# A hybrid decoder trunk on one Trainium2 core: the attention scores of token tile 1, all heads of a pair at once in four banks

## The chip, the cores and the metric

One core of one Trainium2 chip runs the whole program. The metric is the device time of one execution in microseconds (us); the median of several runs is compared. A profiled execution of the kernel before is at hand, and all rows below are from it.

The engines in this text: PE is the matrix engine, ACT the engine of activations and copies (ScalarE), DVE the vector engine, POOL the general one (GpSimd), SP the one that issues the loads. Each works through its own queue in the order in which the program gave it its instructions, and waits for the others by semaphores.

## The reference

Two decoder layers over 256 tokens and 1024 channels in float32. Each layer has a gated feed-forward block, a mixer of two parallel parts, a second feed-forward block and a small gated embedding. One part of the mixer is an mLSTM, the other an attention in which each query sees the 128 newest keys:

```python
def hybrid_layer(h, ...):
    h = h + 0.5 * swiglu(rmsnorm(h, ffn1_norm), ffn1_w_gate, ffn1_w_up, ffn1_w_down)
    z = rmsnorm(h, mix_norm) @ w_in            # mLSTM q k v o i f, attention q k v, two merge gates
    hm = mlstm_chunkwise(...)                  # q and k after a short convolution and SiLU
    ha = swa_gqa_sinks(aq, ak, av, a_sinks)
    h = h + (sigmoid(g_m) * (hm @ w_branch_m) + sigmoid(g_a) * (ha @ w_branch_a)) @ w_out
    h = h + 0.5 * swiglu(rmsnorm(h, ffn2_norm), ffn2_w_gate, ffn2_w_up, ffn2_w_down)
    return h + sigmoid(rmsnorm(h, ple_norm) @ ple_gate_w) * (p_i @ ple_proj_w)

def swa_gqa_sinks(q, k, v, sinks):             # 16 query heads, 4 key heads, blocks of 128 queries
    scores = einsum("bnqhgd,bnkhd->bnhgqk", qb, kw) / 8        # over two blocks of keys
    scores = where(valid, scores, -inf)        # 0 <= query - key < 128
    mx = maximum(max(scores), sink); pr = exp(scores - mx)
    den = sum(pr) + exp(sink - mx)
    return einsum("bnhgqk,bnkhd->bnqhgd", pr / den, vw)
```

## The kernel before

**Tiles.** The tokens are two tiles of 128, `t` = 0 and 1. Activations stand transposed, as channels by tokens. Every float32 factor is split into a high and a low half (`wh` and `wl` for weights, made by `feed` from the loaded `raw`: ACT casts `wh`, DVE subtracts to get `wl`), and a product is three matmuls: high by high, high by low, low by high. A weight part is 128 x 1024; PE needs both halves of a part when it reaches it. The weights ring has 8 parts.

**Order.** The text of the program is executed by a planner. `Clock` holds a model time for each engine from a few fixed costs; background work is written as Python generators (chains), each `yield` ends a stage, and `tick`, called between matmuls of the main jobs, advances every chain whose stage is done by the model time (`chain[1] <= self.clock.now`) and then feeds weight parts, if the model has ACT and DVE not too far behind. So what an edit of a chain does to the order reaches much further than the chain: the stages of all other chains and the weight parts fall to other places. The engines then follow the order as it was written down, whatever the true times are.

**The stretch in question** is the mixer, some 250 us per layer. PE's main jobs stand there in this order: `kvq` (attention q, k, v), `v` (mLSTM values), `gt` (merge gate A; four banks `gt`, read by ACT into `gate`), `if` (mLSTM gates; then `scans` on DVE, with an exponential and a logarithm on ACT), `z` (mLSTM q and k for two heads; two units of four weight parts each, followed by the convolution `conv`: four activations `cv` on ACT, 12 taps on DVE in two stages of six, a SiLU `cy` and a split `qk`), `ya` (the attention's output times its branch weights; reads the attention's result in `qT`), `og`, `z`, `gt`, `ym`, `yo`.

In the background run `scores` for each head pair `p` and tile `t` (started by `groups`), then two chains of `outputs`, each for four heads: exponential of the sink `es`, reciprocal of `dn`, scaling of `pr` on ACT, four transposes into a bank `tp`, split `ptd` (for tile 1 a second, masked `ptd` on DVE), the product `ha`, and its copy `hc`; when both halves of a pair are there, the result is split into `qT`. The decays of the mLSTM (`decays`: bank `wt`, exponentials `w`) run beside them. PSUM has 8 banks in one ring, `bank`, for all of this.

**`scores`** makes S = (t + 1) x 128 keys. A bank holds `per` = 512 / S heads: 4 for tile 0, 2 for tile 1. For tile 1 the loop over `j0` runs twice; each pass makes two banks (`sc`, one for each of two key heads `g`), then a copy of the newer block on ACT, the masked copy of the older block, the maxima on DVE, and the exponentials on ACT with their sums. The second pass begins after the exponentials of the first.

Of the kernel before, what the change touches and what calls it, by code (L numbers as in the profile page):

```python
# [14 lines left out]
AF = mybir.ActivationFunctionType  # L15
ALU = mybir.AluOpType
AX = mybir.AxisListType
PSUM = bass.MemoryType.PSUM

P = 128  # L20
# [12 lines left out]
NEG = -1e30  # L33
# [1228 lines left out]
class Swa:  # L1262
# [95 lines left out]
    def scores(self, t, p, acc, chains):  # L1358


        tr, nc = self.tr, self.nc
        S = (t + 1) * P
        per = NB // S
        tok = slice(t * P, (t + 1) * P)
        rows = [slice(g * AD, (g + 1) * AD) for g in range(2)]
        hd = [slice(4 * (2 * p + g), 4 * (2 * p + g) + 4) for g in range(2)]
        pr = tr.slot("pr")[:, : 8 * P].rearrange("p (g j s) -> p g j s", g=2, j=4)
        pr = [pr[:, g] for g in range(2)]
        mx, den = ([tr.col(n, 4) for _ in range(2)] for n in ("mx", "dn"))
        for j0 in range(0, 4, per):  # L1370
            js = slice(j0, j0 + per)
            ps = [tr.bank("sc").rearrange("p (j s) -> p j s", j=per) for _ in range(2)]
            for j in range(per):
                for x, y in ((0, 0), (0, 1), (1, 0)):
                    for g in range(2):
                        nc.tensor.matmul(ps[g][:, j, :], self.qT[x](4 * p + j0 + j, tok, p=rows[g]),
                                         self.kT[rows[g], y, p, :S], start=j + x + y == 0, stop=x == 1,
                                         skip_group_check=True)
            yield
            if t:  # L1380
                for g in range(2):
                    nc.scalar.copy(pr[g][:, js, :], ps[g][:, :, P:])
                yield
            for g in range(2):
                if t:
                    above = tr.above.bitcast(mybir.dt.uint32)[:, None, :].to_broadcast([P, per, P])
                    nc.vector.copy_predicated(pr[g][:, js, :], above, ps[g][:, :, :P])
                    nc.vector.tensor_reduce(mx[g][:, js], pr[g][:, js, :], axis=AX.X, op=ALU.max)
                else:
                    for j in range(per):  # L1390
                        i = j0 + j
                        nc.vector.tensor_tensor_reduce(pr[g][:, i, :], ps[g][:, j, :], tr.band, 1.0, NEG, op0=ALU.add,
                                                       op1=ALU.max, accum_out=mx[g][:, i : i + 1])
                nc.vector.scalar_tensor_tensor(mx[g][:, js], mx[g][:, js], -0.125, self.nsink[:, hd[g]][:, js],
                                               op0=ALU.mult, op1=ALU.min)
            yield
            for g in range(2):
                for j in range(per):
                    i = j0 + j
                    nc.scalar.activation(pr[g][:, i, :], pr[g][:, i, :], AF.Exp, scale=0.125, bias=mx[g][:, i : i + 1],  # L1400
                                         accum_out=den[g][:, i : i + 1])
        for g in range(2):
            chains.append(tr.later(self.outputs(t, p, g, acc, hd[g], pr[g], mx[g], den[g])))
            self.haT.written(chains[-1], 4 * p, 4, t)
# [76 lines left out]
```

## Time and profile before

| | |
|---|---|
| time, median of 3 runs | 1360.45 us (1360.2 to 1360.47) |
| the profiled execution | 1360.21 us, span 1358.5 us |
| matmuls / weight loads / DVE / ACT / POOL busy | 1350.4 / 1224.4 / 901.2 / 748.6 / 57.4 us |
| ACT table loads | 15, 1.283 us each |

The span runs from the first to the last instruction of the core. A timeline row has the start in us from the span's beginning, its length, engine, line, operation, output <- inputs with their sizes, and how many equal instructions follow each other in it (a row of several is as long as all of them); in brackets the idle time ahead of it and who ended it. A row of the waits gives who waited for whom: us in total, times, longest. Nearly every row has line 133, the recording helper, so work is told apart by its tiles. A matmul's row is longer than the time to the next one, since they overlap.

### The profile page before, as it was taken

Reading aid. Unit: us, or ns where it says so; the run is one execution under the profiler, and the core shown is the slowest. Engines: PE = TensorE matmul, PEld = TensorE weight load, DVE = VectorE, ACT = ScalarE, POOL = GpSimd, SP = SyncE. Lnnn points to the kernel's source line nnn. Section 1 sums busy time; section 2 is a strip of 40 time slices with the busy share of each in tenths; the row PEclk is TensorE's granted clock in tenths of the full one; section 3 lists DMA queues with packets and bytes.
Section 4 is the critical chain, followed back from the end, with each engine's and each line's share of the span. In section 5 each row is a group of like instructions: output and inputs, shape, how many; then the busy total and the mean of one; then the engine's idle time right before and its main releaser. Section 6 shows DMA issues by size and latency. Waiting matters only on the chain.

```text
span 1358.5 us, 22054 instructions
## 1 busy us (share of the span) xinstructions
PE 1350.4 (99%) x8990; PEld 1224.4 (90%) x8990; DVE 901.2 (66%) x1403; ACT 748.6 (55%) x1233; POOL 57.4 (4%) x82
## 2 busy tenths in 40 slices
PE   9999999999999999999999999999999999999998
PEld 7999887899899899988889998878998998999887
DVE  6766567888787655454666554578887876554545
ACT  6655446887565444443555443468875654444433
POOL 1000003000100000000000000020001000000000
PEclk9999999999999999999999999999999999999999
DMA  7655745355654475565466566463546554755651
GB/s 246 219 187 159 247 151 190 122 153 126 214 203 163 153 235 186 174 221 182 166 219 218 171 196 198 139 200 110 159 123 217 198 173 143 243 188 170 237 191 53
DMA packets 126789, 245.91 MB, mean 181 GB/s; under 512 B 15160, under 2 KB 24288, under 8 KB 126688
## 3 DMA queue, kind: packets, MB, share of 16 engines
q1 hardware_dynamic: 126672, 244.50, 55.7%
q8 instruction: 70, 1.15, 0.4%
q14 instruction: 31, 0.25, 0.1%
q10 hardware_dynamic: 16, 0.00, 0.0%
HBM read 242.39 MB, written 2.10 MB: 180 GB/s over the span
## 4 chain that ended last, share of the span: by engine, by line
PE 97%; DVE 2%; ACT 1%; issue 0%; DVEq 0%; ACTq 0%
PE dn L133 18%; PE pg L133 18%; PE pu L133 14%; PE gu L133 7%; PE gt L133 7%; PE z L133 7%; PE kvq L133 5%; PE ym L133 3%; PE og L133 3%; PE yo L133 3%; PE v L133 3%; PE tp L133 3%; PE ya L133 2%; PE sc L133 1%; DVE cv L133 1%; PE ha L133 1%
## 5 line engine op out<-in xcount | busy, mean ns | idle before, releaser
L133 DVE TENSOR_TENSOR wl<-raw,wh 128x1024 fp32r<-128x1024 f32 (+1 forms) x405 | 488.1, 1221 | 275.9 <-ACT wh L133 273.4
L133 ACT CAST wh<-raw 128x1024 fp32r<-128x1024 f32 x405 | 415.7, 1048 | 351.1 <-PE dn L133 68.8
L133 PE MATMUL dn<-wh,hid 128*128 128x512 f32 x688 | 218.1, 395 | 0.0
L133 PE MATMUL pg<-uT,wh 128*128 128x256 f32 x1088 | 195.0, 282 | 0.0
L133 PE MATMUL pu<-uT,wh 128*128 128x256 f32 x1088 | 193.9, 281 | 0.0
L133 PEld LDWEIGHTS pg<-uT,wh 128*128 128x128 f32 x1088 | 166.7, 188 | 0.3
L133 PEld LDWEIGHTS pu<-uT,wh 128*128 128x128 f32 x1088 | 166.3, 188 | 0.0
L133 PEld LDWEIGHTS dn<-wh,hid 128*128 128x128 f32 x688 | 129.2, 188 | 30.3
L133 PE MATMUL pg<-uT,wl 128*128 128x256 f32 x544 | 152.6, 280 | 0.0
L133 PE MATMUL pu<-uT,wl 128*128 128x256 f32 x544 | 152.5, 280 | 0.0
L133 PE MATMUL dn<-wl,hid 128*128 128x512 f32 x352 | 138.9, 395 | 0.0
L133 PEld LDWEIGHTS pg<-uT,wl 128*128 128x128 f32 x544 | 102.7, 189 | 0.0
L133 PEld LDWEIGHTS pu<-uT,wl 128*128 128x128 f32 x544 | 102.7, 189 | 0.0
L133 PE MATMUL gt<-uT,wh 128*128 128x256 f32 x512 | 92.8, 282 | 0.0
L133 PE MATMUL z<-uT,wh 128*128 128x256 f32 x512 | 92.6, 283 | 0.0
L133 PE MATMUL gu<-wh,uT 128*128 128x512 f32 x256 | 81.2, 398 | 0.6 <-ACT wh L133 0.4
L133 PEld LDWEIGHTS gt<-uT,wh 128*128 128x128 f32 x512 | 79.0, 188 | 1.5
L133 PEld LDWEIGHTS dn<-wl,hid 128*128 128x128 f32 x352 | 66.1, 188 | 15.3
L133 PEld LDWEIGHTS z<-uT,wh 128*128 128x128 f32 x512 | 78.8, 188 | 0.6
L133 ACT ACTIVATE wh<-raw,gcol 128x512 fp32r<-128x512 f32 (+1 forms) x104 | 58.9, 638 | 27.5 <-DMA raw<-in_ffn_w_gate_dram 16.1
L133 DVE SCALAR_TENSOR_TENSOR wl<-raw,gcol,wh 128x512 fp32r<-128x512 f32 (+1 forms) x104 | 62.5, 655 | 16.3 <-ACT wh L133 16.0
L133 PE MATMUL z<-uT,wl 128*128 128x256 f32 x256 | 71.9, 281 | 0.0
(221 smaller groups left out, 2178.2 us busy)
## 6 DMA issues: line engine op xcount, KB each, us to landing
raw<-in_w_in_dram SPq DMA_DIRECT2D x60, 1024.0 KB
raw<-in_ffn_w_up_dram SPq DMA_DIRECT2D x40, 1024.0 KB
raw<-in_ffn_w_down_dram SPq DMA_DIRECT2D x40, 1024.0 KB
raw<-in_ffn_w_gate_dram SPq DMA_DIRECT2D x38, 1024.0 KB
raw<-in_w_branch_a_dram SPq DMA_DIRECT2D x16, 512.0 KB
raw<-in_w_branch_m_dram SPq DMA_DIRECT2D x8, 1024.0 KB
raw<-in_w_out_dram SPq DMA_DIRECT2D x8, 1024.0 KB
raw<-in_ple_gate_w_dram SPq DMA_DIRECT2D x8, 1024.0 KB
```

The lines of the kernel that those rows point to most:

```text
L133: return issue(*args, **kw)
```

## The change

For tile 1 the two passes become one: the 24 score matmuls of a head pair stand in one block (they stood in two blocks of 12), in four banks at once instead of two and then two. Then come a stage of four copies on ACT, a stage of all masked copies and maxima on DVE, and a stage of all eight exponentials. Tile 0 has one pass as before; only the way in which its stages are written changes.

```diff
--- before.py
+++ after.py
@@ -1367,38 +1367,37 @@
         pr = tr.slot("pr")[:, : 8 * P].rearrange("p (g j s) -> p g j s", g=2, j=4)
         pr = [pr[:, g] for g in range(2)]
         mx, den = ([tr.col(n, 4) for _ in range(2)] for n in ("mx", "dn"))
+        banks = {}
         for j0 in range(0, 4, per):
-            js = slice(j0, j0 + per)
-            ps = [tr.bank("sc").rearrange("p (j s) -> p j s", j=per) for _ in range(2)]
+            banks[j0] = ps = [tr.bank("sc").rearrange("p (j s) -> p j s", j=per) for _ in range(2)]
             for j in range(per):
                 for x, y in ((0, 0), (0, 1), (1, 0)):
                     for g in range(2):
                         nc.tensor.matmul(ps[g][:, j, :], self.qT[x](4 * p + j0 + j, tok, p=rows[g]),
                                          self.kT[rows[g], y, p, :S], start=j + x + y == 0, stop=x == 1,
                                          skip_group_check=True)
+        yield
+        parts = [(slice(j0, j0 + per), g, ps[g]) for j0, ps in banks.items() for g in range(2)]
+        if t:
+            for js, g, ps in parts:
+                nc.scalar.copy(pr[g][:, js, :], ps[:, :, P:])
             yield
+        for js, g, ps in parts:
             if t:
-                for g in range(2):
-                    nc.scalar.copy(pr[g][:, js, :], ps[g][:, :, P:])
-                yield
-            for g in range(2):
-                if t:
-                    above = tr.above.bitcast(mybir.dt.uint32)[:, None, :].to_broadcast([P, per, P])
-                    nc.vector.copy_predicated(pr[g][:, js, :], above, ps[g][:, :, :P])
-                    nc.vector.tensor_reduce(mx[g][:, js], pr[g][:, js, :], axis=AX.X, op=ALU.max)
-                else:
-                    for j in range(per):
-                        i = j0 + j
-                        nc.vector.tensor_tensor_reduce(pr[g][:, i, :], ps[g][:, j, :], tr.band, 1.0, NEG, op0=ALU.add,
-                                                       op1=ALU.max, accum_out=mx[g][:, i : i + 1])
-                nc.vector.scalar_tensor_tensor(mx[g][:, js], mx[g][:, js], -0.125, self.nsink[:, hd[g]][:, js],
-                                               op0=ALU.mult, op1=ALU.min)
-            yield
-            for g in range(2):
-                for j in range(per):
-                    i = j0 + j
-                    nc.scalar.activation(pr[g][:, i, :], pr[g][:, i, :], AF.Exp, scale=0.125, bias=mx[g][:, i : i + 1],
-                                         accum_out=den[g][:, i : i + 1])
+                above = tr.above.bitcast(mybir.dt.uint32)[:, None, :].to_broadcast([P, per, P])
+                nc.vector.copy_predicated(pr[g][:, js, :], above, ps[:, :, :P])
+                nc.vector.tensor_reduce(mx[g][:, js], pr[g][:, js, :], axis=AX.X, op=ALU.max)
+            else:
+                for j in range(4):
+                    nc.vector.tensor_tensor_reduce(pr[g][:, j, :], ps[:, j, :], tr.band, 1.0, NEG, op0=ALU.add,
+                                                   op1=ALU.max, accum_out=mx[g][:, j : j + 1])
+            nc.vector.scalar_tensor_tensor(mx[g][:, js], mx[g][:, js], -0.125, self.nsink[:, hd[g]][:, js],
+                                           op0=ALU.mult, op1=ALU.min)
+        yield
+        for g in range(2):
+            for j in range(4):
+                nc.scalar.activation(pr[g][:, j, :], pr[g][:, j, :], AF.Exp, scale=0.125, bias=mx[g][:, j : j + 1],
+                                     accum_out=den[g][:, j : j + 1])
         for g in range(2):
             chains.append(tr.later(self.outputs(t, p, g, acc, hd[g], pr[g], mx[g], den[g])))
             self.haT.written(chains[-1], 4 * p, 4, t)
```

The number of matmuls, DVE instructions and ACT instructions other than table loads stays. Where they stand in the queues changes through the planner, in both layers alike. Three places, in the first layer (numbers behind names are the program's own and differ between the two orders):

ACT's queue at the job `gt`, before: the exponentials of tile 1, pair 1 (`pr` with `mx`), the copies of its scores and the gates.

```order
L133 CAST wh_3124<-raw_2986 128x1024
L133 ACTIVATE pr_3036,dn_3039<-pr_3036,mx_3037 128x128 x2
L133 ACTIVATE pr_3036,dn_3040<-pr_3036,mx_3038 128x128 x2
L133 COPY pr_3036<-sc_3144 128x256
L133 COPY pr_3036<-sc_3145 128x256
L133 CAST wh_3174<-raw_3061 128x1024
L133 COPY hc_3183<-ha_3168 64x512
L133 CAST wh_3185<-raw_3061 128x1024
L133 ACTIVATE gate_3200<-gt_2888 128x512
L133 ACTIVATE gate_3200<-gt_2889 128x512
L133 COPY hc_3183<-ha_3217 64x512
L133 ACTIVATE pr_3036,dn_3039<-pr_3036,mx_3037 128x128 x2
```

The same place after the change:

```order
L133 COPY pr_2993<-sc_3012 128x256
L133 COPY pr_2993<-sc_3013 128x256
L133 CAST wh_3052<-raw_2852 128x1024
L133 COPY hc_2972<-ha_3043 64x512
L133 ACTIVATE es_3062<-es_3062 128x4
L133 ACTIVATE es_3064<-es_3064 128x4
L133 CAST wh_3083<-raw_2852 128x1024
L133 ACTIVATE gate_3149<-gt_2835 128x512
L133 ACTIVATE gate_3149<-gt_2836 128x512
L133 ACTIVATE pr_2993,dn_2996<-pr_2993,mx_2994 128x128 x4
L133 ACTIVATE pr_2993,dn_2997<-pr_2993,mx_2995 128x128 x4
L133 CAST wh_3166<-raw_3081 128x1024
```

All eight exponentials now stand behind the two `gate` activations, and with them `qT` and the scaling of tile 0 (`pr` with `dn`); four of them stood ahead of the gates.

DVE's queue at the job `z`, before: the taps `cv` of the first unit (`z` is its bank), the masked `ptd`, and the weight halves `wl` near them.

```order
L133 TENSOR_TENSOR wl_3438<-raw_3306,wh_3437 128x1024
L133 TENSOR_TENSOR ptd_3446<-tp_3432,ptd_3446 128x512
L133 TENSOR_TENSOR ptd_3497<-ptd_3430,upto 128x512 x2
L133 SCALAR_TENSOR_TENSOR cv_3465<-z_3302,feat_2151,cv_3465 128x255
L133 SCALAR_TENSOR_TENSOR cv_3465<-z_3302,feat_2151,cv_3465 128x254
L133 SCALAR_TENSOR_TENSOR cv_3465<-z_3302,feat_2151,cv_3465 128x253
L133 SCALAR_TENSOR_TENSOR cv_3468<-z_3303,feat_2151,cv_3468 128x255
L133 SCALAR_TENSOR_TENSOR cv_3468<-z_3303,feat_2151,cv_3468 128x254
L133 SCALAR_TENSOR_TENSOR cv_3468<-z_3303,feat_2151,cv_3468 128x253
L133 TENSOR_TENSOR rows_93<-nM_3301,rows_93 4x384
L133 TENSOR_TENSOR ptd_3525<-ptd_3446,upto 128x512 x2
L133 TENSOR_TENSOR wl_3482<-raw_3306,wh_3481 128x1024
```

After the change:

```order
L133 TENSOR_TENSOR ptd_3388<-tp_3367,ptd_3388 128x512
L133 TENSOR_TENSOR hc_3381<-ha_3383,hc_3381 64x512
L133 SCALAR_TENSOR_TENSOR cv_3441<-z_3268,feat_2151,cv_3441 128x255
L133 SCALAR_TENSOR_TENSOR cv_3441<-z_3268,feat_2151,cv_3441 128x254
L133 SCALAR_TENSOR_TENSOR cv_3441<-z_3268,feat_2151,cv_3441 128x253
L133 SCALAR_TENSOR_TENSOR cv_3444<-z_3269,feat_2151,cv_3444 128x255
L133 SCALAR_TENSOR_TENSOR cv_3444<-z_3269,feat_2151,cv_3444 128x254
L133 SCALAR_TENSOR_TENSOR cv_3444<-z_3269,feat_2151,cv_3444 128x253
L133 TENSOR_TENSOR rows_93<-nM_3267,rows_93 4x384
L133 TENSOR_TENSOR ptd_3477<-ptd_3386,upto 128x512 x2
L133 TENSOR_TENSOR ptd_3486<-ptd_3388,upto 128x512 x2
L133 TENSOR_TENSOR wl_3490<-raw_3275,wh_3489 128x1024
```

`wl_3490` is the low half of the sixth of the eight weight parts of `z`. In the order before, `wl_3438` and `wl_3482` at the same place belong to `ya`; all parts of `z` stand further ahead, the sixth ahead of the scans. Now the taps, `rows` and both masked `ptd` pairs stand between the scans and the sixth part of `z`.

ACT's queue between `z` and `ya`, before: `cy` is the SiLU, `em` and `w` are exponentials, which need another table.

```order
L133 ACT_TABLE_LOAD
L133 ACTIVATE cy_3620<-cv_3465 128x512
L133 ACTIVATE cv_3629<-z_3471,feat_2151 128x256 x2
L133 ACTIVATE cv_3632<-z_3472,feat_2151 128x256 x2
L133 ACTIVATE cy_3646<-cv_3468 128x512
L133 ACT_TABLE_LOAD
L133 ACTIVATE em_3654<-gcols_3588 128x8
L133 CAST qk_3658<-cy_3620 128x512
L133 CAST qk_3660<-cy_3646 128x512
L133 CAST qT_140<-hc_3558 128x4x128
L133 ACTIVATE w_3681<-wt_3656,gcols_3588 128x128 x3
```

After the change:

```order
L133 ACT_TABLE_LOAD
L133 ACTIVATE cy_3549<-cv_3441 128x512
L133 ACT_TABLE_LOAD
L133 ACTIVATE em_3566<-gcols_3538 128x8
L133 CAST qk_3570<-cy_3549 128x512
L133 ACT_TABLE_LOAD
L133 ACTIVATE cy_3572<-cv_3444 128x512
L133 CAST wh_3578<-raw_3494 128x1024
L133 CAST qT_140<-hc_3535 128x4x128
L133 CAST wh_3598<-raw_3494 128x1024
L133 ACT_TABLE_LOAD
L133 ACTIVATE w_3590<-wt_3568,gcols_3538 128x128 x3
```

The two `cy` stood together in one table; they now stand apart, with exponentials between them, and each change of function has a table load. The whole order has 23 of them, where the one before has 15: four more in each layer, all behind the logarithm.

## The prediction

> **What bounds the kernel now.** I read the page first, then the waits of the matrix engine (PE), the busy times of the mixer's middle, and its timelines.
>
> ```profile
> span 1358.5 us, 22054 instructions
> PE 1350.4 (99%) x8990; PEld 1224.4 (90%) x8990; DVE 901.2 (66%) x1403; ACT 748.6 (55%) x1233; POOL 57.4 (4%) x82
> PE 97%; DVE 2%; ACT 1%; issue 0%; DVEq 0%; ACTq 0%
> ```
>
> PE is busy for 99% of the span and is 97% of the chain that ended last. The change keeps PE's 8990 matmuls, so it can gain little more than PE's idle time, 1358.5 - 1350.4 = 8.1 us; it can lose whatever PE is made to wait.
>
> ```profile
> PE ya L133 <- DVE wl L133: 0.9, 2, 0.5
> 285.00:305.00 20.00, 20.00 (x172) 20.00 (x171) 16.95 (x36) 16.46 (x38) 0.00 (x0) 1.00 0.56 142
> 305.00:325.00 20.00, 20.00 (x163) 19.49 (x162) 17.06 (x32) 12.33 (x21) 0.00 (x0) 1.00 0.59 124
> ```
>
> The first row is from the waits, the others from the busy times in stretches (PE, weight loads, DVE, ACT, POOL, granted clock, DMA share, GB/s). In the middle of the mixer DVE is busy 17 of each 20 us and ACT 12 to 16. This is the one stage where these two nearly set the pace: `ya` already waits for a `wl` half, once per layer (0.9 us, 2 times). An order that makes them idle for some us here can't win that back.
>
> **The change part by part.** The work on each engine is equal but for the table loads below. What counts is where the planner now puts it.
>
> *1. Joined score blocks (a gain).* Two blocks of 12 score matmuls become one of 24, twice per layer.
>
> ```profile
> 240.97 0.98 PE L133 MATMUL sc<-kT,qT 64*128 64x256 f32 x12
> 241.87 0.50 PE L133 MATMUL v<-wh,uT 128*128 128x512 f32 x1
> 251.92 1.09 PE L133 MATMUL ha<-ptd,vv 128*128 128x512 f32 x4
> 252.85 0.40 PE L133 MATMUL v<-wh,uT 128*128 128x512 f32 x1
> 274.51 0.60 PE L133 MATMUL tp<-ident,pr 128*128 128x128 f32 x4
> ```
>
> Twelve take 0.90 us from start to start. Entering and leaving a block shows as a matmul's 0.50 where 0.40 is usual, and as much ahead: 0.2 us a joint. Two joints, and some transposes that now stand side by side, save 0.7 us per layer (between 0 and 1).
>
> *2. Banks.* The four score banks and the four of `gt` are all eight. Six `gt` matmuls later the order has `ha_3043`, which needs a score bank back: a copy on ACT and a masked copy on DVE must end first, on DVE behind a `wl` split of 1.2 us. Between 0 and 1.2 us; I take 0.8, as both engines have other work in front.
>
> *3. Wait A, at the `z` weights.* ACT's queue now has the two `gate` activations ahead of the eight exponentials of tile 1 (first place shown in the order); before, four of these stood ahead of the gates. ACT stands idle until PE ends the bank of `gt_2835`, and all behind it starts then.
>
> ```profile
> 281.43 2.85 PE gt L133 x24
> 290.91 8.51 PE z L133 x72
> 301.01 7.80 PE z L133 x66
> ```
>
> These are rows of the chain that ended last. The 24 are the 133rd to 156th `gt` matmul; the bank is full with the 138th: 281.4 + 6 x 0.118 + 0.2 for the result = 282.3. By the order of the changed kernel PE has two blocks of transposes less ahead of it (the row at 274.51, 0.60 with a tail of about 0.25, so 0.35 each), a pair of `ha` (half of 0.93) and two joints (0.4), 1.6 us together, and the 0.8 of the bank more: 281.5, say 281.4.
>
> ```profile
> 232.16 0.40 ACT L133 ACTIVATE pr<-pr,mx 128x128 f32<-128x128 f32 x1
> 235.26 0.62 ACT L133 COPY pr<-sc 128x256 f32<-128x256 f32 x2
> 271.49 2.45 ACT L133 ACTIVATE pr<-pr,dn 128x128 f32<-128x128 f32 x8
> 283.25 1.09 ACT L133 ACTIVATE gate<-gt 128x512 f32<-128x512 f32 x2
> 286.94 1.99 ACT L133 CAST wh<-raw 128x1024 fp32r<-128x1024 f32 x2
> 289.79 0.61 ACT L133 CAST qT<-hc 128x512 fp32r<-128x512 f32 x1
> 290.30 0.30 ACT L133 ACTIVATE es<-es 128x4 f32<-128x4 f32 x2
> 293.73 1.28 ACT L133 ACT_TABLE_LOAD   x1
> 295.02 0.42 ACT L133 ACTIVATE gates<-gates 4x256 f32<-4x256 f32 x1
> 301.32 0.59 ACT L133 CAST ptd<-tp 128x512 fp32r<-128x512 f32 x1
> ```
>
> ACT then runs, by its order, without a pause to the logarithm of the gates (start to start, in us): gates 1.05, eight exponentials 3.10 (232.16 to 235.26), `wh` 1.0, `qT` 0.5, eight scalings 2.4, `wh` 1.0, `es` 0.2, gates 1.05, `wh` 1.0, two `ptd` 1.0, `wh` 1.0, eight scalings 2.4, exponential 0.4, table 1.28, logarithm 0.42: 17.8. So it ends at 299.2, where before it ended at 295.44.
>
> ```profile
> 288.00 2.36 DVE L133 TENSOR_TENSOR wl<-raw,wh 128x1024 fp32r<-128x1024 f32 x2 [1.56 <-ACT wh L133]
> 295.47 0.41 DVE L133 SCALAR_TENSOR_TENSOR gates<-gates,gates 4x256 f32<-4x256 f32 x1
> 299.14 1.21 DVE L133 TENSOR_TENSOR wl<-raw,wh 128x1024 fp32r<-128x1024 f32 x1
> 302.59 0.69 DVE L133 TENSOR_TENSOR ptd<-tp,ptd 128x512 fp32r<-128x512 f32 x1
> 303.19 1.29 DVE L133 TENSOR_TENSOR ptd<-ptd,upto 128x512 fp32r<-128x512 f32 x2
> 304.39 2.93 DVE L133 SCALAR_TENSOR_TENSOR cv<-z,feat,cv 128x255 f32<-128x255 f32 x6
> 307.34 0.55 DVE L133 TENSOR_TENSOR rows<-nM,rows 4x384 fp32r<-4x384 f32 x1
> ```
>
> DVE goes on (second place in the order): the scans 3.67 (295.47 to 299.14), `wl` 1.2, two `hc` and two `ptd` at 0.6 (302.59 to 303.19), six taps of `cv` 2.95, `rows` 0.55, four masked `ptd` 2.4 (1.2 a pair), `wl_3490` 1.2: 14.4, so 313.6. PE needs `wl_3490` in the sixth of eight weight parts of `z`. In the order before, the sixth part is split by 290.4 (the row at 288.00), 16 us ahead. PE gets there after 120 `z` matmuls: 72 and 6 (not shown), then 42 of the 66, 301.0 + 5.0 = 306.0, and two matmuls with the high half follow at 306.2. The work ahead of it is the same in both orders, so in the changed kernel 306.2 + 0.8 - 0.7 = 306.3. Wait A: 7.3 us; the summed queues are good to a tenth of 32 us, so 4 to 10. Rows that follow each other overlap by up to 0.1, so the sum is a little long; I take 6.8.
>
> *4. Wait B, at the `ya` weights.* Exponential and SiLU need different tables. The order has 23 table loads where the page's groups had 15: four more per layer, all after the logarithm (third place).
>
> ```profile
> L133 ACT ACT_TABLE_LOAD x15 | 19.2, 1283 | 5.0 <-DVE cv L133 3.4 <-PEq L1470 1.4
> 302.47 1.93 ACT L133 ACTIVATE cv<-z,feat 128x256 f32<-128x256 f32 x4 [0.56 <-PE z L133]
> 317.82 0.63 ACT L133 ACTIVATE cy<-cv 128x512 f32<-128x512 f32 x1
> 322.22 1.12 ACT L133 CAST qk<-cy 128x512 fp32r<-128x512 f32 x2
> 323.77 0.87 ACT L133 ACTIVATE w<-wt,gcols 128x128 f32<-128x128 f32 x3
> ```
>
> After A ends at t, PE does 4 `z`, 8 `ha` (first four done at t + 1.7), the small transposes, 66 `z`, two `wt`, 50 `ya`: 0.5 + 1.9 + 0.3 + 7.8 + 0.6 + 5.9 + 0.5 for joints = 17.5 until `ya` needs `wl_3665`. ACT, starting from `ha`: two copies to t + 3.2, then `wh` 1.0, four tables 5.1, two `cy` 1.1, two `qk` 1.0, `qT` 0.5, two `wh` 2.0, `w` 0.8, first `cv` pair 0.95: t + 15.65; DVE then six taps 2.95 and the split 1.2: t + 19.8. Wait B is 2.3 (0 to 4). The next part, `wl_3682`, follows six more taps and a split, 4.15 later, while PE has 3.3 of work: wait C, 0.85. Without the two extra tables of this stretch (2.6 us), B would be nothing. The other two load while ACT has time.
>
> *5. The clock after A.*
>
> ```profile
> 1354.00:1356.00 2.00, 0.35 (x3) 0.14 (x2) 0.85 (x2) 0.38 (x1) 0.00 (x0) 1.00 0.02 7
> 1356.00:1358.50 2.50, 0.00 (x0) 0.00 (x0) 0.00 (x0) 0.00 (x0) 0.00 (x0) 0.60 0.15 52
> 1.68 2.32 PE L568 MATMUL heat<-heat 128*128 128x512 bf16 x5 [1.68 <-DVE heat L563]
> 5.55 0.59 PE L568 MATMUL heat<-heat 128*128 128x512 bf16 x2
> ```
>
> PE ends at 1354.35, and the granted clock falls to a mean of 0.60 in the last 2.5 us, so about 2 us of rest lower it. At the start 512 columns take 0.46 us, by 5.55 about half; the slow spell lasts 2.3 to 3.9 us. A wait of 6.8 us should set this off; the PE then loses half the spell, 1.2 to 1.9 us. C and B could hide it, but their `ha` is slowed as well. I take 1.5 (0 to 2) per layer. The Trainium skill's TensorE: Matmul & The Clock Gate, section Why this matters for your kernels, warns of gaps over about 3 us. By that rule B's 2.3 lowers nothing and A does, which is the sum as it stands.
>
> **Sum per layer:** bank 0.8, A 6.8, B 2.3, C 0.85, clock 1.5, less the joints 0.7 and the old `ya` wait 0.45: 11.1. Both layers have the same order, so 22.2. The profiled execution took 1360.21 (1.7 us outside the span), 0.24 below the median of the three runs: 1360.45 + 22.2 = 1382.7, say 1383.
>
> **The rivals.**
> - *The clock stays up:* 1383 - 3 = 1380. The end of the trace speaks against it.
> - *A is hidden.* If ACT's and DVE's queues regain their lead before `z`, B, C and bank remain without the clock: 2 x (0.8 + 2.3 + 0.85 - 1.15) = 5.6, so 1366. For it: DVE is 3 us of 20 idle before. Against: the idle time stands ahead of the gates, and the queue behind is unbroken by the order.
> - *The lag goes on:* ACT reaches the `og` weights and the mLSTM heads late too, one more wait like B and C: 2 x 5, so 1393. For it: four loads too many; against: in the second half of `ya` its order holds little but weight halves.
> - *A table load costs twice its row*, by a stall around it: 1.28 more for one load in A and four in B, 2 x 6.4 more, 1396. Against: the load at 293.73 is followed by the logarithm at 295.02, 1.29 later. The Trainium skill's ScalarE: Activation LUTs, section What ACT_TABLE_LOAD costs, adds a drain of about 1.38 us to each load; this trace has none.
> - *Not slower.* Only the joints count: 1360.45 - 2 x 1.15 = 1358. This needs the queue from the gates to `wl_3490` to run in 24.9 us instead of 32.2; it decides at 306.3. That is 23% off a sum of measured rows.
>
> **How the numbers follow.** Forecast with the clock's fall 0.5, without it 0.25, hidden A 0.08, lag that goes on 0.11, dear table loads 0.02, not slower 0.04. Likeliest is 1383. With A at 4 and no clock it is 1374, A at 10 gives 1389; with a part of the hidden case below and the lag above, 1370 to 1394. A change under 0.2% (2.7 us) can't be told from none: faster 0.02, same 0.02, slower 0.96.
>
> **What would show it.** PE's waits would list `z` behind DVE `wl`, twice, 5 to 8 us each, and `ya` behind DVE `wl` at 2 to 3; the granted clock would dip near 315 and 995. ACT should idle 3 to 5 us ahead of `gate`. The table loads would count 23. If `z` doesn't wait, or PE's idle time stays near 8 us, the argument is wrong.

## The result, and the profile after

The changed kernel takes 1386.03 us (median of 4 runs, 1385.51 to 1386.65) against 1360.43 for the kernel before: 1.0186 times as long, with a 95% interval of 1.0174 to 1.0198. It is 25.6 us slower, where the forecast had 22.2; the time lies inside the forecast range, 1383 (1370 to 1394). The profiled execution took 1385.95, with a span of 1384.2: 25.7 more than before.

The page, the table loads from its groups, and the waits of PE (what PE waited for and which engine ended it; us in total, times, the longest):

```profile
span 1384.2 us, 22068 instructions
PE 1354.4 (98%) x8990; PEld 1226.6 (89%) x8990; DVE 900.5 (65%) x1403; ACT 758.8 (55%) x1241; POOL 49.9 (4%) x82
PE 93%; DVE 3%; ACT 2%; issue 0%; DMA 0%; SPq 0%; ACTq 0%
L133 ACT ACT_TABLE_LOAD x23 | 29.5, 1283 | 10.7 <-DVE cv L133 9.0 <-PEq L1469 1.4
PE z L133 <- DVE wl L133: 12.9, 2, 6.5
PE ya L133 <- DVE wl L133: 7.2, 6, 2.1
PE ha L133 <- DVE pr L133: 1.9, 2, 1.0
PE gu L133 <- ACT wh L133: 1.2, 2, 1.0
```

The work is the same, 8990 matmuls. PE's idle time is 1384.2 - 1354.4 = 29.8 us where it was 8.1, and DVE and ACT now hold 5% of the chain that ended last, where they held 3%. The list names the places: once per layer `z` waits 6.5 us for a weight half, `ya` waits three times, `ha` waits 1.0 for a score bank.

The first layer in the timelines, PE's rows first:

```profile
274.32 1.20 PE L133 MATMUL ha<-ptd,vv 128*128 128x512 f32 x4 [0.97 <-DVE pr L133]
314.24 0.58 PE L133 MATMUL z<-uT,wl 128*128 128x256 f32 x1 [6.43 <-DVE wl L133]
315.26 3.62 PE L133 MATMUL ha<-ptd,vv 128*128 128x512 f32 x8
328.74 0.38 PE L133 MATMUL ya<-qT,wl 128*128 128x256 f32 x1 [0.76 <-DVE wl L133]
337.07 0.39 PE L133 MATMUL ya<-qT,wl 128*128 128x256 f32 x1 [2.15 <-DVE wl L133]
341.05 0.39 PE L133 MATMUL ya<-qT,wl 128*128 128x256 f32 x1 [0.72 <-DVE wl L133]
282.02 1.25 ACT L133 ACTIVATE gate<-gt 128x512 f32<-128x512 f32 x2 [4.62 <-PE gt L133]
295.10 2.45 ACT L133 ACTIVATE pr<-pr,dn 128x128 f32<-128x128 f32 x8
297.88 1.28 ACT L133 ACT_TABLE_LOAD   x1
299.17 0.42 ACT L133 ACTIVATE gates<-gates 4x256 f32<-4x256 f32 x1
312.97 1.22 DVE L133 TENSOR_TENSOR wl<-raw,wh 128x1024 fp32r<-128x1024 f32 x1
331.48 1.96 ACT L133 ACTIVATE cv<-z,feat 128x256 f32<-128x256 f32 x4
331.81 0.63 DVE L133 TENSOR_TENSOR wt<-wt,mask_st 128x128 f32<-128x128 f32 x2 [1.39 <-PE wt L133]
```

The brackets give the idle time ahead of a row and what ended it. ACT rests 4.62 us ahead of the gates, the logarithm ends at 299.6 (forecast 299.2), `wl_3490` is split at 314.2 (forecast 313.6), and PE, idle since 307.8, goes on at 314.24. The same weight part was split by 290.4 before: it now comes 24 us later. The last two rows are ahead of the second wait at `ya`: DVE's masking of `wt` waits 1.39 us for PE.

Stretches around that wait (busy us of PE, weight loads, DVE, ACT, POOL; then the granted clock, DMA share, GB/s):

```profile
310.00:312.00 2.00, 0.00 (x0) 0.00 (x0) 1.99 (x4) 0.00 (x0) 0.00 (x0) 1.00 0.00 0
312.00:313.00 1.00, 0.00 (x0) 0.00 (x0) 1.00 (x3) 0.00 (x0) 0.00 (x0) 0.83 0.00 0
313.00:319.00 6.00, 4.76 (x14) 3.53 (x15) 4.50 (x9) 0.67 (x2) 0.00 (x0) 0.50 0.53 128
319.00:320.00 1.00, 1.00 (x9) 0.98 (x9) 0.46 (x2) 0.97 (x2) 0.00 (x0) 0.76 1.04 201
```

At half speed the clock stands for 0.34 + 6 + 0.48 = 6.8 us. It falls near 312.7, 4.9 us after PE went idle, and is back near 319.5, 5.2 us after PE went on; the eight `ha` in that spell take 3.62 us.

### The profile page after: what moved, and what is told of

Same layout as the page of the kernel before. It is cut to its first block, busy times and chain, and to the rows that moved or that the text cites. A ratio compares the mean times of both kernels' runs of the same rounds, so it can differ in the third digit from the quotient of the medians.

```text
span 1384.2 us, 22068 instructions
## 1 busy us (share of the span) xinstructions
PE 1354.4 (98%) x8990; PEld 1226.6 (89%) x8990; DVE 900.5 (65%) x1403; ACT 758.8 (55%) x1241; POOL 49.9 (4%) x82
## 3 DMA queue, kind: packets, MB, share of 16 engines
q8 instruction: 70, 1.15, 0.3%
## 4 chain that ended last, share of the span: by engine, by line
PE 93%; DVE 3%; ACT 2%; issue 0%; DMA 0%; SPq 0%; ACTq 0%
PE dn L133 17%; PE pg L133 17%; PE pu L133 14%; PE gu L133 7%; PE gt L133 6%; PE z L133 5%; PE kvq L133 5%; PE ym L133 3%; PE og L133 3%; PE yo L133 3%; PE v L133 3%; PE ya L133 2%; PE tp L133 2%; DVE cv L133 1%; PE ha L133 1%; DVE wl L133 1%
```

## The experiments

All ratios are to the kernel before, run on the same chip beside each (medians of 1360.60 to 1360.76).

**tables: no switching of tables.** SiLU of the mLSTM convolution is left out, Tanh stands in its place; the planner still counts it as SiLU, so the order stays.

```
-        nc.scalar.activation(y, acc.rearrange("p c t -> p (c t)"), AF.Silu)
+        y_in = acc.rearrange("p c t -> p (c t)")
+        tr.clock.charge("scalar", NB, AF.Silu)
+        tr.tc.nc.scalar.activation(y, y_in, AF.Tanh)
```

> The order of the changed kernel, instruction for instruction, but the last activation of the mLSTM convolution (cy) is issued as Tanh, which shares its table with the exponential; SiLU of the convolution is left out. The extra table loads of the middle are gone, so the loads fall well under 15. Theory 1 (step 4 of the prediction): the table loads make the waits at ya; without them the three waits of 0.76, 2.15 and 0.72 us per layer go, 1386.0 - 2 x 3.6 = 1378.8, at least the 2.15, 1381.7. Theory 2: the wait of 2.15 is set by DVE, whose masking of wt waits 1.39 us for PE's own wt at 331.4 and has 0.6 + 0.6 + 2.9 + 1.2 us behind it until wl; then only the 0.76 behind the first ya goes, all behind it moves with PE, the waits of 2.15 and 0.72 stay: 1386.0 - 1.5 = 1384.5. The wait at z stays at 6.4 under both, since only one load, that of the logarithm, lies ahead of it and stays.

Measured: 1384.50 us, ratio 1.0173 (1.0158 to 1.0188). The page lists 9 table loads (7 and 2, on two lines of the kernel) where the changed kernel has 23. PE's waits, PE's row of wait B, and DVE ahead of it:

```profile
PE z L133 <- DVE wl L133: 12.9, 2, 6.5
PE ya L133 <- DVE wl L133: 5.9, 4, 2.2
337.51 0.39 PE L133 MATMUL ya<-qT,wl 128*128 128x256 f32 x1 [2.24 <-DVE wl L133]
332.25 0.63 DVE L133 TENSOR_TENSOR wt<-wt,mask_st 128x128 f32<-128x128 f32 x2 [3.92 <-PE wt L133]
332.79 0.68 DVE L133 TENSOR_TENSOR qk<-cy,qk 128x512 fp32r<-128x512 f32 x1
333.39 2.93 DVE L133 SCALAR_TENSOR_TENSOR cv<-z,feat,cv 128x255 f32<-128x255 f32 x6
336.24 1.22 DVE L133 TENSOR_TENSOR wl<-raw,wh 128x1024 fp32r<-128x1024 f32 x1
```

Theory 2 holds. The 0.76 goes, the 2.15 stays as 2.24. With 14 loads less DVE only rests longer, 3.92 us, in front of the masking of `wt`, which waits for PE's own `wt`; the split that `ya` needs stands behind that mask and six taps. So wait B (the 2.15) is a fixed distance in DVE's queue behind a PE instruction. The median falls by 1.5 us, and the intervals of the two kernels overlap. That is not the price of the 14 loads alone: in the first layer the clock stays at half speed twice as long here (last section), so that from the `z` matmul to the first `ya` PE takes 329.02 - 313.89 = 15.13 us where the changed kernel takes 327.54 - 314.24 = 13.30. The spans of the two profiled executions differ by 1.2 us; with this 1.83 added, the loads are worth about 3 us, an estimate. Of the 3.92 us of rest, at least about 2.1 would be left without the longer spell, so the mask would wait for PE all the same.

**fill44 and fill20: PE kept busy in the wait.** Matmuls with a zero weight, 44 in one run and 20 in the other, are put ahead of the `z` matmul that waits; they add nothing to `z`. The main lines, as in fill44:

```
                     mm(o, part.hi[:, kk - k0, cc], xT[1](kk), start=False, stop=False, **kw)
+                    if base == "z" and c == 0 and kk == 2:
+                        self.fills += 1
+                        for _ in range(44 if self.fills % 4 == 2 else 0):
+                            self.tc.nc.tensor.matmul(o, self.zero, xT[0](kk), start=False, stop=False, **kw)
```

> The changed kernel with 44 matmuls with a zero weight, 0.118 us each, that add nothing to z, put ahead of the z matmul that waits for wl in each layer: PE is busy for 5.2 of the 6.43 us that it waits. Theory 1: the clock falls because PE rests; it then stays at 1.00, the 6.83 us at 0.5 are gone, the wait at z is listed as 1.2, and PE gains most of the 2.6 us per layer: 1386.0 - 5.2 = 1380.8, and up to 1382 if a part is given back. Rival 1: the lost clock was hidden anyway, the waits at ya grow from 3.6 to 6.2 per layer: 1386. Rival 2: the clock falls for another reason: 0.5 is there again after the wait, 1386.

> As fill44 with 20 zero matmuls, 2.4 us, at the front of the wait: PE rests for 4.0 us behind them instead of 6.43. In the changed kernel the clock fell 4.9 us after PE had gone idle. Theory 1: it falls only after about that much rest, so here it stays at 1.00 and the time is that of fill44, 1381 to 1382. Rival: a rest of about 3.4 us (half of the 6.83 us that the record shows at 0.5) or less is enough, the clock falls to 0.5 as before, the time stays at 1386.

Measured: fill44 1382.17 us, 1.0156 (1.0141 to 1.0171); fill20 1385.84 us, 1.0183 (1.0168 to 1.0198). PE's rows of fill44 with one of its stretches, then of fill20 with two:

```profile
307.41 5.30 PE L504 MATMUL z<-uT,zero 128*128 128x256 f32 x44
314.00 0.38 PE L133 MATMUL z<-uT,wl 128*128 128x256 f32 x1 [1.30 <-DVE wl L133]
326.46 0.38 PE L133 MATMUL ya<-qT,wl 128*128 128x256 f32 x1 [0.76 <-DVE wl L133]
334.79 0.38 PE L133 MATMUL ya<-qT,wl 128*128 128x256 f32 x1 [2.16 <-DVE wl L133]
300.00:320.00 20.00, 18.70 (x149) 17.85 (x148) 19.39 (x39) 11.14 (x18) 0.00 (x0) 1.00 0.36 101
```

```profile
306.83 2.50 PE L504 MATMUL z<-uT,zero 128*128 128x256 f32 x20
313.42 0.58 PE L133 MATMUL z<-uT,wl 128*128 128x256 f32 x1 [4.09 <-DVE wl L133]
310.00:312.00 2.00, 0.00 (x0) 0.00 (x0) 2.00 (x4) 0.00 (x0) 0.00 (x0) 0.96 0.00 0
312.00:314.00 2.00, 0.58 (x2) 0.58 (x3) 2.00 (x4) 0.00 (x0) 0.00 (x0) 0.50 0.00 0
```

With 44 the clock stays up, and from the `z` matmul to the first waiting `ya` PE takes 326.46 - 314.00 = 12.46 us where the changed kernel takes 328.74 - 314.24 = 14.50. That is the price of the fall in the first layer, 2.04 us. In the second the same stretch takes 1015.73 - 1003.29 = 12.44 and 1019.44 - 1005.34 = 14.10, so 1.66. The waits at `ya` behind it are unchanged (0.76, 2.16), so nothing is given back. In medians it is 3.9 us for both layers, with intervals that lie just apart: less than theory 1's 5.2, and 0.2 above its 1382. With 20 the clock falls all the same, after 2.5 us of rest in the first layer, and the time is that of the changed kernel: theory 1's figure of 4.9 us was wrong.

**swap: the gates behind the exponentials.** On ACT alone, the two `gate` activations of the first two `gt` banks are kept back and issued right behind the eight exponentials of tile 1.

```
-                nc.scalar.activation(two(out, k), ps, AF.Tanh, scale=0.5)
+                if c0 == C_GA and k < 4:
+                    self.clock.charge("scalar", NB, AF.Tanh)
+                    o = two(out, k)
+                    self.behind.append(lambda: self.tc.nc.scalar.activation(o, ps, AF.Tanh, scale=0.5))
+                else:
+                    nc.scalar.activation(two(out, k), ps, AF.Tanh, scale=0.5)
...
+        while t and tr.behind:
+            tr.behind.pop(0)()
```

> The changed kernel with one pair of rows moved on ACT in each layer: the two gate activations stand behind the eight exponentials of tile 1 instead of ahead of them; every other engine's order is equal. Theory 1 (step 3 of the prediction): ACT's rest of 4.62 us ahead of the gates and the unbroken queue behind it set the wait at z; the exponentials (3.1 us) can start when the maxima end (277.8) and fill the rest, the logarithm ends 3 us sooner, the wait at z is 3.4, too short for the clock to fall: 1386.0 - 2 x (3.0 + 2.6) = 1374.8. Theory 2: the queue has a second hold, the scalings at 295.10, which start when DVE's dn ends at 295.27, behind the gates from PE's if at 292.40, which nothing here moves; then the logarithm ends where it did, the wait at z stays above 5.5 and the clock falls: 1384 to 1386.

Measured: 1383.42 us, 1.0165 (1.0148 to 1.0182). ACT's rows, DVE's row that holds them, and PE's:

```profile
281.67 1.24 ACT L956 ACTIVATE gate<-gt 128x512 f32<-128x512 f32 x2 [1.48 <-PE gt L133]
293.44 2.45 ACT L133 ACTIVATE pr<-pr,dn 128x128 f32<-128x128 f32 x8 [1.77 <-DVE dn L133]
290.75 0.47 DVE L133 TENSOR_SCALAR gates<-if,m_igate_b 4x256 f32<-4x256 f32 x1 [1.83 <-PE if L133]
312.60 0.58 PE L133 MATMUL z<-uT,wl 128*128 128x256 f32 x1 [5.61 <-DVE wl L133]
```

ACT's rest ahead of the gates shrinks from 4.62 to 1.48, but a rest of 1.77 opens ahead of the scalings: they need DVE's `dn`, which stands behind the gates that wait for PE's `if`. Wait A goes from 6.43 to 5.61, the clock still falls. The two kernels' intervals overlap, so the gain of 2.6 us is not settled; that A stays above 5.5 is. Theory 2 is right about the hold, and its 1384 is missed by 0.6.

**mm_only and stages_only: each part alone.**

```
mm_only, against the changed kernel:
-        parts = [(slice(j0, j0 + per), g, ps[g]) for j0, ps in banks.items() for g in range(2)]
+        for j0, ps in banks.items():
+            js = slice(j0, j0 + per)
+            if j0:
+                yield
...
stages_only, against the changed kernel:
         for j0 in range(0, 4, per):
+            if j0:
+                yield
             banks[j0] = ps = [tr.bank("sc").rearrange("p (j s) -> p j s", j=per) for _ in range(2)]
```

In mm_only copies, maxima and exponentials then stand inside that loop, as in the kernel before; in stages_only other work can come between the two blocks of matmuls.

> One part alone: the 24 score matmuls of tile 1 in one block into four banks, as in the changed kernel; copies, maxima and exponentials in two passes of two banks each, as in the kernel before. In its order 162 weight parts are split on DVE ahead of the rows split in the first layer (163 in the kernel before, 159 in the changed one). Theory 1 (the single stages of copies, maxima and exponentials move the other work, and the weight parts fall behind): without them no wait at z above 1 us, the clock stays at 1.00, the joints bring up to 0.7 per layer, waits at ya of up to 1: 1359 to 1363. Theory 2 (four banks taken at once is what costs): most of the loss stays, above 1372, with waits at ha, gt or z.

> The other part alone: copies, maxima and exponentials of tile 1 take one stage each, as in the changed kernel; the matmuls stay in two blocks of 12 with other work between them. In its order 162 weight parts are split ahead of rows. Theory 1 (single stages cost by themselves, through the weight parts that fall behind): 3 parts more than in the changed kernel are split in time, so no long wait at z and no fall of the clock, but waits at ya of 3 to 6 us per layer: 1367 to 1375. Theory 2 (only both together cost): 1359 to 1363. Theory 3 (the eight exponentials in one run on ACT are the whole cause): 1380 to 1386 with the wait at z.

Measured: mm_only 1358.29 us, 0.9983 (0.9974 to 0.9992), faster than both kernels, by an interval that stays below 1; stages_only 1379.72 us, 1.0137 (1.0120 to 1.0154). The longest wait of mm_only in the layers, then the waits of stages_only at `ya`:

```profile
PE gu L133 <- ACT wh L133: 0.9, 2, 0.7
```

```profile
PE ya L133 <- ACT wh L133: 8.2, 2, 4.1
PE ya L133 <- DVE wl L133: 3.0, 4, 1.1
```

The joined matmuls alone make no wait above 0.7 and bring 2.5 us, 0.7 more than theory 1's best case. PE's busy time is 1348.7 us, 1.7 less than before, so most of the gain lies in PE's own work, as the joints would have it. The joined stages alone cost 19 us, by waits of 5.6 us per layer at `ya` (4.1 for a high half, 1.5 for low halves) and a clock that falls in that gap; the waits are 11 of the 19. `z` does not wait. So theory 1 of stages_only was right on the place, but missed the clock, and the time lies above its range.

**exps_joined: one stage joined.** mm_only, with the eight exponentials in one stage behind both passes of copies and maxima.

```
-            yield
+        yield
+        for j0, ps in banks.items():
+            js = slice(j0, j0 + per)
             for g in range(2):
                 for j in range(per):
...
```

> mm_only with one more step towards the changed kernel: the 24 matmuls in one block, copies and maxima in two passes of two banks, and then all eight exponentials of tile 1 in one stage. 163 weight parts ahead of rows, as in the kernel before. Theory 1 (the joined exponentials are what delays the rest): waits at ya of 3 to 5 us per layer, perhaps with the clock, 1366 to 1374, most of the way from mm_only (1358.3) to stages_only (1379.7). Theory 2 (the joined copies and maxima are): the weight parts are on time, no wait above 1 us, 1357 to 1361.

Measured: 1372.24 us, 1.0082 (1.0066 to 1.0097). Its waits:

```profile
PE ya L133 <- DVE qT L133: 5.0, 2, 2.5
PE ya L133 <- ACT qT L133: 2.3, 2, 1.2
PE ya L133 <- DVE cv L133: 1.1, 2, 0.6
```

Theory 1 holds on the price: the joined exponentials take 1372.2 - 1358.3 = 14 us back. Yet it is not the weights that are late here but the attention's own result `qT`, 3.7 us per layer, with 0.5 more behind `cv` and a fall of the clock (its mean is 0.995, in mm_only 1.000). Joining the copies and maxima as well adds the other 14 us, up to 1386.0, and moves the long wait from `ya` to `z`.

**after_feed and before_feed: the same edit in another order.** Both kernels with the planner's slack for weight parts changed.

```
-AHEAD = (3.0, 2.0)
+AHEAD = (3.4, 3.0)
```

> The changed kernel with AHEAD = (3.4, 3.0) for (3.0, 2.0): the planner may take in a weight part while its ACT or DVE clock is up to 3.4 (3.0 with four parts in store) us ahead of PE. In its order 162 weight parts are split ahead of rows, for 159 in the changed kernel. Theory 1 (the loss is that weight parts are taken in too late for z, not the score work itself): no wait at z above 1 us, no fall of the clock, a wait at ya of about 2 us per layer stays, and a bank wait of about 1: 1360.5 + 2 x 3 = 1364 to 1368. Theory 2 (the joined stages keep ACT and DVE too late whatever the feeding): waits at z or ya of 8 us or more per layer in all: above 1376.

> The kernel before with the same AHEAD = (3.4, 3.0), the partner of after_feed: 166 weight parts ahead of rows. If the edit costs by itself, this stands 20 us or more below after_feed; if the price of the edit is the order that the planner happens to make, within 5 us of it, 1362 to 1367, with a wait at ya of about 2 us per layer.

Measured: after_feed 1368.37 us (1367.24 to 1375.62), 1.0067 (1.0041 to 1.0093); before_feed 1364.44 us, 1.0030 (1.0019 to 1.0041). The waits of after_feed, then of before_feed:

```profile
PE ya L133 <- DVE qT L133: 3.5, 2, 1.8
PE sc L133 <- ACT v L133: 2.9, 2, 1.5
```

```profile
PE ya L133 <- DVE qT L133: 2.9, 2, 1.6
```

With these numbers `z` no longer waits, and the edit costs 3.9 us instead of 25.6 (the two intervals just touch). The time of after_feed is 0.4 us above theory 1's range, and in its profiled execution, the slowest of its four, the clock fell four times during PE's work, which theory 1 had excluded. So most of the edit's price is the order that the planner makes with one pair of constants. The kernel before, too, loses 3.7 us by the new pair.

**mm_haste: a version meant to beat both.** mm_only with one constant changed, `STORE, HASTE = 4, 4` for `4, 3`.

> mm_only with HASTE = 4 for 3, so that weight parts are taken in up to four in store while the norm is hurried; a version that may beat both kernels. In mm_only PE waits 0.9 us in two places at gu for ACT's wh. Theory 1: these 0.9 us go, 1357.4. Theory 2: the parts then stand ahead of the norm's own work on ACT, which PE waits for instead: 1358.3 or more.

Measured: 1358.10 us, 0.9982 (0.9973 to 0.9990): the same as mm_only. The `gu` wait for `wh` is gone, `tp` waits 0.5 for `xn` instead. So the wait moved as theory 2 said, but the two times can't be told apart.

## Why the prediction was right, point by point

What the runs showed in the first layer, beside the terms of the sum per layer:

| term | forecast | first layer | from |
|---|---|---|---|
| joints and the old `ya` wait | -1.15 | -1.2 | mm_only, half of 2.47 us for two layers |
| bank wait at `ha` | 0.8 | 0.97 | row at 274.32 |
| wait A at `z` | 6.8 | 6.43 | row at 314.24 |
| waits at `ya` (B and C) | 2.3 + 0.85 | 0.76 + 2.15 + 0.72 | rows at 328.74 to 341.05 |
| clock | 1.5 | 2.0 | fill44 |
| sum | 11.1 | 11.8 | |

The second layer makes 11.4, mostly for its smaller price of the clock, 1.66. Together that is 23.2 of the 25.7 us between the spans, and `gu` waits 0.8 more for ACT's `wh` (1.2, before 0.4). The last 1.7 us are not assigned.

- **Wait A** came at the place and, to half a us, at the size forecast, since the sum of queued rows held: 299.6 for 299.2 at the logarithm, 314.2 for 313.6 at the split. What the step made of it was too simple. It put the idle time ahead of the gates at the root; swap took 3.1 us of that away and A lost 0.8, because the scalings are held a second time by `dn` behind PE's `if`. What the runs point to is the place of the weight parts. The split that `z` waits for is DVE's 160th of the program. It ends at 290.4 in the kernel before, 289.7 in exps_joined, 296.6 in mm_only, 299.3 in stages_only and 300.0 in after_feed, none of which waits at `z`, and at 314.2 in the changed kernel, where PE needs it at 307.8. By the orders the changed kernel has split 159 parts when `rows` is split in the first layer, the others 162 or 163. That agrees, but no run moved a weight part alone, so the cause stays open to that extent. And it would explain wait A only: exps_joined and stages_only have the part in time and still lose 12 and 19 us, at `ya`.
- **Waits B and C** were sized right for a wrong reason: 2.15 and 0.72 for 2.3 and 0.85. "Without the two extra tables of this stretch (2.6 us), B would be nothing" is the step that failed: with 14 loads less, B was 2.24. The sum went from `ha` along ACT; the release that ends last is PE's `wt`, through DVE's mask and six taps. The size was luck in part, since the two paths nearly meet: ACT's first `cv` pair ends near 332.5 (half of the row at 331.48), and the taps start at 332.95, behind the mask. The loads made a wait that the sum did not have, the 0.76 ahead of B, which goes without them. The rival of dear table loads falls: it asked for 12.8 us more, and all 14 loads are worth about 3 (estimated above). mm_only, too, has 21 loads where the kernel before has 15, and is the faster one. The Trainium skill's drain of about 1.38 us with each load (ScalarE: Activation LUTs, What ACT_TABLE_LOAD costs) is not seen in the changed kernel either: the logarithm starts at 299.17, 1.29 us after its load at 297.88.
- **The clock** was undersized: 1.5 (0 to 2) forecast, 2.04 and 1.66 measured in the two layers. The slow spell was taken from the start of the trace as 2.3 to 3.9 us; it was 6.8, of which 5.2 with PE at work in the first layer and 3.6 in the second.
- **The rivals.** The clock did not stay up; A was not hidden; the lag did not go on past `ya`, as no wait at `og` is listed. "Not slower", 1358 by the joints alone, is what mm_only gives: 1358.3. So the price of the joints was about right (0.85 us of PE's busy time per layer for 0.7), and with the planner's constants as they stand the joined stages are what turned the change into a loss.

## What to carry to other kernels

Where a planner sets the order, an edit of one chain is priced by what it moves: here, with fewer and larger stages, the weight parts or the attention's own result came too late for the matrix engine, and another pair of the planner's constants took most of that price away. Join the matmuls, which save their joints, apart from the stages of the engines behind them, and time each alone. Follow a wait back to the release that ends last, past the busiest queue, before giving its price to an instruction in that queue.

## What the runs showed of the hardware

When the clock falls, and for how long, hung on more than the length of the wait. Three stretches around wait A of tables, then a wait of after_feed with two stretches behind it:

```profile
308.00:310.00 2.00, 0.00 (x0) 0.00 (x0) 1.92 (x5) 0.37 (x1) 0.00 (x0) 0.89 0.00 0
320.00:322.00 2.00, 2.00 (x11) 2.00 (x11) 1.94 (x4) 1.97 (x3) 0.00 (x0) 0.50 0.12 24
322.00:324.00 2.00, 2.00 (x14) 2.00 (x13) 1.07 (x1) 2.00 (x5) 0.00 (x0) 0.70 0.00 0
261.61 1.52 PE L133 MATMUL sc<-kT,qT 64*128 64x128 f32 x23 [1.46 <-ACT v L133]
262.00:266.00 4.00, 4.00 (x35) 3.93 (x33) 3.90 (x20) 1.39 (x5) 0.00 (x0) 0.66 0.01 4
266.00:268.00 2.00, 2.00 (x17) 2.00 (x16) 1.97 (x6) 2.00 (x13) 0.00 (x0) 0.83 0.00 0
```

The first three rows are of the first layer of tables: PE is idle since 307.5, its clock falls at 309.6, 2.1 us later, and is back only at 323.2, 13.6 us at half speed. In the first layer of the changed kernel it fell after 4.9 us of the same wait, in that of fill20 after 2.5, for 6.8 us each; in fill20's second layer the spell was 3.4 us (means of 0.68, 0.50 and 0.96 in the three stretches of 2 us from 1004). In after_feed a wait of 1.46 us is followed by 2.7 + 0.7 = 3.4 us at half speed, and the other three falls during PE's work in that execution follow waits of 2.20, 1.49 and 1.77 us, whereas waits of 2.15 and 2.24 at `ya`, in the changed kernel and in tables, lowered nothing. The spells are one, two or four times 3.4 us. That agrees with a free-running window of about 3.4 us, which the Trainium skill describes in TensorE: Matmul & The Clock Gate, Part 1: The HAM clock gate; its advice against gaps over about 3 us, in the section Why this matters for your kernels, is no safe bound here, as the 1.46 us shows. How much rest in such a window lowers the clock stays open.

The spells differ from one execution of a kernel to the next: the mean clock of the changed kernel was 0.992 to 0.995 in its four, and the profiled one of after_feed took 1375.6 us where its others took 1367.2 to 1368.7.
